# Stick-breaking logits: zero-padded products against two 64-row products

## The chip, the cores and the metric

One core of one Trainium2 chip runs the whole program. The metric is the device time of one execution in microseconds. An engine is named by the profile's short names: PE multiplies matrices (PEld is its weight load), DVE is VectorE, ACT is ScalarE, POOL is GpSimd, SP issues most of the DMAs.

## The reference

Two transformer blocks run one after the other over 512 tokens of width 1024, all in float32. The first block's mixer has two halves of 8 heads of 64: RWKV-7 (a recurrence over time) and stick-breaking attention. Then come an output projection and 32 experts, two for each token. The second block has HGRN-2 and forgetting attention as its mixer, and 16 experts. The change touches stick-breaking attention, and only its first product:

```python
z = jnp.einsum('bhqd,bhkd->bhqk', qb, kb) * scale        # d = 64, blocks of 128 queries
log_rest = jnp.where(strict, jax.nn.log_sigmoid(-z), 0.0)
suffix = lax.cumsum(log_rest, axis=3, reverse=True) - log_rest
weights = jnp.where(strict, jnp.exp(jax.nn.log_sigmoid(z) + suffix), 0.0)
outs.append(jnp.einsum('bhqk,bhkd->bhqd', weights, vb))
```

Block b reads the keys up to its own end, so 128, 256, 384 or 512 of them.

## The kernel before, in words

The program is written as one long list of instructions, and a planner orders it. It keeps a queue for each engine, takes what is ready first by its place in the program, and so moves instructions far ahead of the place where they are written, as long as their data and their buffers allow it. `in_order` (L214) holds the instructions traced inside it to their written order on each engine; other instructions may still be put between them.

`mixer1` (L443) begins with the norm and the transposed input `xh`, `xl`. A projection (`proj`, L310) is 24 matmuls of 512 columns with weights `w` that SP loads in 0.5 MB pieces into three buffers; ACT and DVE split each piece into `whi` and `wlo`. `mixer1_rw_in` (L533) makes the RWKV inputs from 14 projections. Its first step after two projections reads `lw`, 0.5 MB of LoRA weights (loaded at L538, used by the matmuls of L561 and L564, whose results go through sigmoids on ACT). Then follow steps in the order `R00 R01 P0 R10 R11 A0 P1 R20 R21 A1 P2 R30 R31 A2 P3 A3`. An R step is a unit of RWKV (`rw_unit`, many small matmuls, some of them on 64 rows). P steps (`sb_proj`, L645) make queries, keys and values of head pair j: three projections. A steps (`sb_attn`, L660) are the attention of a head pair.

In `sb_proj` the queries of a pair go into `qz`, 128 rows by 2 heads by 512: head 0 stands in rows 0 to 63 of the first half, head 1 in rows 64 to 127 of the second, and two memsets on POOL (L648, L649) zero the rest. `kT` holds the keys of both heads in its 128 rows. So a product of 128 rows (L672) gives the logits of one head, the other head's rows being multiplied by zeros. It starts the accumulation in a PSUM bank; a product of the identity with the mask `causx` (L673) ends it. A float32 product is two passes on PE. From the bank DVE takes the smaller of logit and 80 into `sbz` (L675). There are two banks for all this, `sb`, taken in turn by the scores, the transposed weights, the outputs and the head norm. `qz`, `kT` and `vS` have two buffers each, so pair j shares those of pair j - 2.

At P2 the kernel also clears `yd` (L500 to L504), a buffer in DRAM of 5 MB into which the first block's experts are added much later. The source of this DMA is one of the zeroed halves of `qz`: rows 64 to 127 of the first head of pair 2, repeated along `yd`.

Of the kernel before, what the change touches and what calls it, by code (L numbers as in the profile page):

```python
# [8 lines left out]
F32 = mybir.dt.float32  # L9
# [3 lines left out]
AF = mybir.ActivationFunctionType  # L13
# [3 lines left out]
T = 512  # L17
# [17 lines left out]
def drain(gen):  # L35

    while True:
        try:
            next(gen)
        except StopIteration as e:  # L40
            return e.value
# [141 lines left out]
class Kern:  # L183
# [259 lines left out]
    def mixer1(self, after):  # L443
        nc, tc = self.nc, self.tc
        cO, cL, cA, cB = ExitStack(), ExitStack(), ExitStack(), ExitStack()
        o = self.pool("m1o", 1, cL).tile([128, KD, T], F32, name="o", tag="o")
        cP = ExitStack()
        xp = self.pool("m1x", 1, cP, "right")
        pp = self.pool("m1p", 1, cP, "right")
        xh = xp.tile([128, KD, T], R32, name="xh")  # L450
        xl = xp.tile([128, KD, T], R32, name="xl")
        sp = self.pool("m1s", 1, cL)
        ap = self.pool("m1a", 1, cA)
        AR = ap.tile([128, 4, NT, 2, 128], F32, name="AR")
        bt = ap.tile([128, 4, T], F32, name="bt")
        kt = ap.tile([128, 4, T], F32, name="kt")
        vch = ap.tile([128, 4, T], F32, name="vch")
        xg = ap.tile([128, T], F32, name="xg")
        TTc = ap.tile([128, C, 8, NT], F32, name="TTc")
        PC = ap.tile([128, 4, 16], F32, name="PC")  # L460
        lora = self.ap["lora"].rearrange("p (a b) -> p a b", a=3)
        xv = self.ap["x"].rearrange("(n p) d -> p n d", p=128)
        self.psum(mm=2, ua=2, ch=1, pq=1, sb=2)
        self.ps_names(pj=("mm", "mm", "sb", "sb"), at=("ua", "ua", "ch", "pq"), tr=("ua", "ua", "ch", "pq"))
        self.proj_plan(self.ap["win"], range(26))
        with ExitStack() as cN:
            p = self.norm_in(self.pool("m1n", 1, cN), pp, xv, xh, xl)
        self.consts(sp, "m1")
        self.causx = self.cbf(sp, "causx")
        bp = self.pool("m1b", 1, cB)  # L470
        self.mixer1_rw_in(bp, bp, pp, p, xh, xl, AR, bt, kt, vch, xg, TTc, PC, lora)
        cB.close()
        up = self.pool("m1u", 1, cA)
        g2 = up.tile([128, 512], F32, name="g2")
        nc.sync.dma_start(g2, lora[:, 2])
        self.ps_names(pj=("mm", ))
        S = [[up.tile([128, 2, 64], F32, name=f"S{g}{i}") for i in range(2)] for g in range(2)]
        for g in range(2):
            nc.vector.memset(S[g][0], 0.0)
        qkv, before = {}, iter(())  # L480

        def shift_pools():
            cP.close()
            self.h = self.pool("hres", 1, None, "right").tile([128, NT, D], F32, name="h")
            self.crow = ExitStack()
            nrow = self.pool("rows", 1, self.crow, "right")
            self.st = nrow.tile([128, 4, NT], F32, name="st")
            self.ring_open(1)
            self.mo.ring[3] = nrow
            wo = self.wo_load(self.ap["wout"])  # L490
            for n in range(NT):
                nc.sync.dma_start(self.h[:, n], xv[:, n])
            return wo


        for step in "R00 R01 P0 R10 R11 A0 P1 R20 R21 A1 P2 R30 R31 A2 P3 A3".split():
            kind, j = step[0], int(step[1])
            if kind == "P":
                qkv[j] = self.sb_proj(pp, sp, j, xh, xl)
                if j == 2:  # L500
                    self.yd = tc.dram_tile([ZROW[1], D], F32, name="yd1")
                    zeros = qkv[j][0][64:128, 0]
                    nc.sync.dma_start(self.yd.rearrange("(p a) (d c) -> p (a d) c", p=64, c=T),
                                      zeros[:, None, :].to_broadcast([64, ZROW[1] // 32, T]))  # L504
                if j == 3:
                    wo = shift_pools()
            elif kind == "A":
                self.sb_attn(sp, j, qkv.pop(j), o, ("sb",))
            else:
                g = int(step[2])  # L510
                unit = self.rw_unit(up, j, g, S[g], o, AR, bt, kt, vch, xg, g2, TTc, PC)
                next(unit)
                drain(before)
                next(unit)
                before = unit
                if (j, g) == (3, 1):
                    drain(unit)
                    cA.close()
        st = self.out_start(o, wo, (0, 1, 2, 4, 5, 6, 7), (3,), (("mm", "mm"), ("ua", "ua"), ("ch", "pq")), cO)
        self.dbg("o", o)  # L520
        cL.close()
        after(st)
        self.out_finish(st, "mm", "sb", ("ch", "ua", "ua", "pq"))
        cO.close()
# [119 lines left out]

    def sb_proj(self, pp, tp, j, xh, xl):  # L645
        nc = self.nc
        qz = tp.tile([128, 2, T], F32, name="qz", bufs=2)
        nc.gpsimd.memset(qz[64:128, 0], 0.0)  # L648
        nc.gpsimd.memset(qz[0:64, 1], 0.0)  # L649
        p = self.proj(pp, 14 + 3 * j, xh, xl)  # L650
        for hh in range(2):
            s = slice(64 * hh, 64 * hh + 64)
            nc.scalar.activation(qz[s, hh], p[s], AF.Copy, scale=0.125)
        kT = tp.tile([128, T], F32, name="kT", bufs=2)
        nc.scalar.activation(kT, self.proj(pp, 15 + 3 * j, xh, xl), AF.Copy)
        vS = tp.tile([128, NT, 128], F32, name="vS", bufs=2)
        self.to_tok(tp, self.proj(pp, 16 + 3 * j, xh, xl), vS, "sb")
        return qz, kT, vS

    def sb_attn(self, tp, j, qkv, o, tags):  # L660


        nc = self.nc
        qz, kT, vS = qkv
        ot = tp.tile([128, T], F32, name="hno", bufs=1)

        def scores(b):
            N = 128 * (b + 1)
            w = []
            for hh in range(2):  # L670
                p = self.rot(tags)
                nc.tensor.matmul(p[:, :N], qz[:, hh, b * 128:(b + 1) * 128], kT[:, :N], start=True, stop=False)  # L672
                nc.tensor.matmul(p[:, N - 128:N], self.identb, self.causx, start=False, stop=True)  # L673
                z = tp.tile([128, T], F32, name="sbz", bufs=2)
                nc.vector.tensor_scalar(z[:, :N], p[:, :N], 80.0, None, op0=OP.min)  # L675
                e = tp.tile([128, T], F32, name="sbe", bufs=2)
                nc.scalar.activation(e[:, :N], z[:, :N], AF.Exp)
                nc.scalar.activation(e[:, :N], e[:, :N], AF.Ln, bias=self.eps[:, 2:3])
                S = tp.tile([128, T], F32, name="sbS", bufs=4)
                nc.vector.tensor_tensor_scan(out=S[:, :N][:, ::-1], data0=self.eps[:, 2:3].to_broadcast([128, N]),  # L680
                                             data1=e[:, :N][:, ::-1], initial=0.0, op0=OP.mult, op1=OP.add)
                nc.vector.tensor_tensor(S[:, :N], z[:, :N], S[:, :N], OP.subtract)
                nc.scalar.activation(S[:, :N], S[:, :N], AF.Exp)
                w.append(S)
            return w

        self.blocks(scores, lambda b, w: self.weighted(tp, tags, b, w, vS, ot))
        self.head_norm(tp, tags, ot, o[:, j], self.c("sbg", j, j + 1))

    def blocks(self, scores, weighted):  # L690

        w = scores(NT - 1)
        for b in reversed(range(NT)):
            nx = scores(b - 1) if b else None
            weighted(b, w)
            w = nx
# [1354 lines left out]
```

## Time and profile before

| | |
|---|---|
| median of 3 runs | 1418.19 us (1415.84 to 1419.23) |
| the profiled execution | 1419.25 us, span 1417.5 us |
| PE busy | 1291.9 us (91% of the span) |
| DVE, ACT, POOL busy | 838.1, 701.4, 409.8 us |
| mean granted clock of PE | 0.964 |

A matmul is shown longer than the time by which it holds back the next one; the distance of the starts is what counts. "x2" in a row of the timeline means two instructions in one stretch. The granted clock is a share of 2.4 GHz.

### The profile page before, as it was taken

To read this page: it belongs to the slowest core of one execution; us is meant where nothing else is said; L and a number is where in the kernel's file an instruction comes from. 1 tells how busy PE (TensorE), PEld (TensorE's weight loads), DVE (VectorE), ACT (ScalarE), POOL (GpSimd) and SP (SyncE) were. 2 spreads that over 40 slices of the span, in tenths; PEclk is the share of its full clock that TensorE was granted. 3 is DMA by queue.
4 is the path that set the end of the run, shared out by engine and by line. 5 is a ranking of instruction groups with operands and counts; after the bars stand their busy time and mean duration, and the time that the engine had idled before them with its cause. 6 is when DMAs were issued, how large, how long until landed. Compare 5 with 4: busy or idle time off the path is not lost.

```text
span 1417.5 us, 20480 instructions
## 1 busy us (share of the span) xinstructions
PE 1291.9 (91%) x7792; PEld 930.9 (66%) x7792; DVE 838.1 (59%) x1432; ACT 701.4 (49%) x1217; POOL 409.8 (29%) x329
## 2 busy tenths in 40 slices
PE   7999999999998899999469899999997999999993
PEld 5776766766697555554257677777795666666662
DVE  4578867556556222000065756566736898898895
ACT  6533433243644122221164555555545788888883
POOL 1000134242103101110357102010124455555455
PEclk9999999999999899999879999999997999999997
DMA  5222350000485999999922121212286999889943
GB/s 189 75 83 81 94 123 2 1 1 1 162 324 194 360 418 420 417 419 420 259 87 76 45 75 34 87 31 88 78 363 224 315 365 382 316 337 390 385 150 143
DMA packets 54452, 283.93 MB, mean 200 GB/s; under 512 B 8849, under 2 KB 9745, under 8 KB 28738
## 3 DMA queue, kind: packets, MB, share of 16 engines
q1 hardware_dynamic: 43634, 254.75, 48.0%
q0 software_dynamic: 9840, 26.39, 5.9%
q8 instruction: 66, 1.08, 0.3%
q10 hardware_dynamic: 864, 1.31, 0.3%
q14 instruction: 48, 0.39, 0.1%
HBM read 270.70 MB, written 22.29 MB: 207 GB/s over the span
## 4 chain that ended last, share of the span: by engine, by line
PE 69%; DVE 12%; DMA 11%; ACT 3%; issue 2%; POOL 1%; SPq 0%; DVEq 0%; POOLq 0%; ACTq 0%
PE mm L322 13%; PE ua L1911 4%; PE ua L1909 4%; PE ua L1910 4%; PE mm L1719 4%; DMA ew<-in_e1down_dram 3%; DMA ew<-in_e1up_dram 3%; PE ua L1663 2%; PE sb L322 2%; PE sb L1852 2%; PE sb L1851 2%; PE sb L1853 2%; PE sb L715 2%; DMA ew<-in_e1gate_dram 2%; DVE elo L1633 1%
## 5 line engine op out<-in xcount | busy, mean ns | idle before, releaser
L1633 DVE TENSOR_TENSOR elo<-ew,ehi 128x1024 fp32r<-128x1024 f32 x147 | 229.6, 1603 | 31.7 <-ACT ehi L1632 20.5
L1632 ACT ACTIVATE ehi<-ew 128x1024 fp32r<-128x1024 f32 x192 | 202.5, 1058 | 59.7 <-PE ua L1910 41.0
L322 PE MATMUL mm<-xh,whi 128*128 128x512 f32 (+1 forms) x384 | 156.7, 408 | 4.0 <-DVE hq L1147 3.7
L322 PE MATMUL mm<-xl,whi 128*128 128x512 f32 (+1 forms) x384 | 154.4, 402 | 0.5 <-DVE xl L354 0.3
L322 PE MATMUL mm<-xh,wlo 128*128 128x512 f32 (+1 forms) x384 | 153.2, 399 | 0.0
L1633 POOL TENSOR_TENSOR elo<-ew,ehi 128x1024 fp32r<-128x1024 f32 x45 | 124.5, 2767 | 63.0 <-ACT ehi L1632 60.9
L1719 PE MATMUL mm<-ew,xTh 128*64 128x256 f32 x1024 | 118.9, 386 | 6.3 <-DMA ew<-in_e1up_dram 4.6
L1911 PE MATMUL ua<-elo,xTh 128*96 128x512 f32 x256 | 103.1, 403 | 8.4 <-DVE elo L1633 8.4
L1719 PEld LDWEIGHTS mm<-ew,xTh 128*64 128x64 f32 x1024 | 73.5, 139 | 47.2 <-DMA ew<-in_e1up_dram 5.9
L1723 DVE TENSOR_TENSOR hh<-hh,mm 128x256 f32<-128x256 f32 x16 | 6.7, 421 | 163.1 <-ACT hh L1722 163.1
L1909 PE MATMUL ua<-ehi,xTh 128*96 128x512 f32 x256 | 102.3, 400 | 0.6 <-ACT xTh L1621 0.6
L1910 PE MATMUL ua<-ehi,xTl 128*96 128x512 f32 x256 | 102.1, 399 | 0.0
L296 ACT ACTIVATE whi<-w 128x1024 fp32r<-128x1024 f32 x53 | 55.9, 1056 | 92.5 <-PE mm L322 73.8
L297 DVE TENSOR_TENSOR wlo<-w,whi 128x1024 fp32r<-128x1024 f32 x52 | 63.8, 1228 | 51.7 <-ACT whi L296 51.5
L1604 POOL DMA_INDIRECT xg<-xd,idx x32 | 36.4, 1138 | 196.5 <-PE sb L1617 118.7
L322 PEld LDWEIGHTS mm<-xh,whi 128*128 128x128 f32 x384 | 74.0, 193 | 23.4 <-DVE hq L1147 5.4
L322 PEld LDWEIGHTS mm<-xl,whi 128*128 128x128 f32 x384 | 74.1, 193 | 16.8 <-issue 3.5
L322 PEld LDWEIGHTS mm<-xh,wlo 128*128 128x128 f32 x384 | 74.1, 193 | 16.1 <-issue 2.2
L1663 PE MATMUL ua<-ew,hT 128*64 128x512 f32 x240 | 66.4, 600 | 1.2 <-ACT hT L1774 1.1
L1911 PEld LDWEIGHTS ua<-elo,xTh 128*96 128x96 f32 x256 | 42.0, 164 | 30.2 <-DVE elo L1633 11.2
L1722 ACT ACTIVATE hh<-mm 128x256 f32<-128x256 f32 x16 | 6.1, 383 | 112.4 <-PE mm L1719 112.4
L1171 POOL TENSOR_TENSOR hAT<-hAT,hmt 128x512 f32<-128x512 f32 x16 | 22.1, 1381 | 119.0 <-DVE hmt L1170 118.4
(640 smaller groups left out, 3034.2 us busy)
## 6 DMA issues: line engine op xcount, KB each, us to landing
ew<-in_e1up_dram SPq DMA_DIRECT2D x32, 1024.0 KB
ew<-in_e2up_dram SPq DMA_DIRECT2D x32, 1024.0 KB
ew<-in_e2gate_dram SPq DMA_DIRECT2D x32, 1024.0 KB
ew<-in_e2down_dram SPq DMA_DIRECT2D x32, 1024.0 KB
ew<-in_e1gate_dram SPq DMA_DIRECT2D x31, 1024.0 KB
ew<-in_e1down_dram SPq DMA_DIRECT2D x30, 1024.0 KB
w<-in_win_dram SPq DMA_DIRECT2D x53, 512.0 KB
ew<-in_wout_dram SPq DMA_DIRECT2D x8, 1024.0 KB
```

Of the source, the lines that this page charges most:

```text
L296: nc.scalar.activation(hi, s, AF.Copy)
L297: (eng or nc.vector).tensor_tensor(lo, s, hi, OP.subtract)
L322: mm = lambda w, x, start=False, stop=False: nc.tensor.matmul(p[:, s], w[:, k], x[:, k, s], start=start, stop=stop, skip_group_check=parts ...
L715: nc.tensor.matmul(po[d, 0:128], v[:, kb, d], wT[hh][:, kb * 128:(kb + 1) * 128], start=kb == 0, stop=kb == b)
L1604: return self.nc.gpsimd.indirect_dma_start(out=xg, out_offset=None, in_=mo.xd, in_offset=bass.IndirectOffsetOnAxis(ap=idx[:, u:u + 1], axi ...
L1632: self.hi = nc.scalar.activation(hi, s, AF.Copy)
L1633: self.lo = (nc.gpsimd if pool else nc.vector).tensor_tensor(lo, s, hi, OP.subtract)
L1663: nc.tensor.matmul(p[hs(a)], hT[:, k, hs(a)], w[a][:, k * 1024 + d * 512:k * 1024 + d * 512 + 512], start=k == 0, stop=k == 1)
L1719: nc.tensor.matmul(d[hs(a)], xT[:, k, hs(a)], w[2 * m + a][:, k * 256:k * 256 + 256], start=k == 0, stop=k == KD - 1)
L1909: nc.tensor.matmul(p, xh[:, kk], hi[:, s], start=kk == 0, stop=False)
L1910: nc.tensor.matmul(p, xl[:, kk], hi[:, s], start=False, stop=False)
L1911: nc.tensor.matmul(p, xh[:, kk], lo[:, s], start=False, stop=kk == KD - 1)
```

## The change

The queries of both heads go into one tile `qT` of 128 rows, unpadded. A new function `products` gives both heads' logits of a block: it takes two banks, starts both with the mask, and then adds for each head a product over its own 64 rows, all held in order. The memsets go, and two copies on ACT become one. The fill of `yd` gets a source of its own, `zrow`, 64 rows of zeros, written by a memset where the fill is issued. The forgetting attention of the second block keeps its padded form.

```diff
                 if j == 2:
                     self.yd = tc.dram_tile([ZROW[1], D], F32, name="yd1")
-                    zeros = qkv[j][0][64:128, 0]
+                    zeros = sp.tile([64, T], F32, name="zrow", bufs=1)
+                    nc.gpsimd.memset(zeros, 0.0)
                     nc.sync.dma_start(self.yd.rearrange("(p a) (d c) -> p (a d) c", p=64, c=T),
                                       zeros[:, None, :].to_broadcast([64, ZROW[1] // 32, T]))
...
     def sb_proj(self, pp, tp, j, xh, xl):
         nc = self.nc
-        qz = tp.tile([128, 2, T], F32, name="qz", bufs=2)
-        nc.gpsimd.memset(qz[64:128, 0], 0.0)
-        nc.gpsimd.memset(qz[0:64, 1], 0.0)
-        p = self.proj(pp, 14 + 3 * j, xh, xl)
-        for hh in range(2):
-            s = slice(64 * hh, 64 * hh + 64)
-            nc.scalar.activation(qz[s, hh], p[s], AF.Copy, scale=0.125)
+        qT = tp.tile([128, T], F32, name="qT", bufs=2)
+        nc.scalar.activation(qT, self.proj(pp, 14 + 3 * j, xh, xl), AF.Copy, scale=0.125)
...
         def scores(b):
             N = 128 * (b + 1)
             w = []
-            for hh in range(2):
-                p = self.rot(tags)
-                nc.tensor.matmul(p[:, :N], qz[:, hh, b * 128:(b + 1) * 128], kT[:, :N], start=True, stop=False)
-                nc.tensor.matmul(p[:, N - 128:N], self.identb, self.causx, start=False, stop=True)
+            for p in self.products(qT, kT, b, self.causx, tags):
                 z = tp.tile([128, T], F32, name="sbz", bufs=2)
...
+    def products(self, q, k, b, mask, tags):
+
+        nc = self.nc
+        N = 128 * (b + 1)
+        banks = [self.rot(tags) for _ in range(2)]
+        with self.in_order():
+            for p in banks:
+                nc.tensor.matmul(p[:, N - 128:N], self.identb, mask, start=True, stop=False, skip_group_check=True)
+            for hh, p in enumerate(banks):
+                s = slice(64 * hh, 64 * hh + 64)
+                nc.tensor.matmul(p[:, :N], q[s, b * 128:(b + 1) * 128], k[s, :N], start=False, stop=True, skip_group_check=True)
+        return banks
```

## Rows read from the trace of the kernel before

**Rows 1.** Busy time by stretch: PE, PEld, DVE, ACT, POOL, granted clock, DMA, GB/s

```profile
31.00:43.00 12.00, 12.00 (x40) 7.26 (x39) 3.68 (x4) 9.94 (x14) 0.20 (x1) 1.00 0.00 0
43.00:118.00 75.00, 74.31 (x356) 58.32 (x355) 54.39 (x88) 29.79 (x42) 7.29 (x12) 1.00 0.29 87
...
170.00:370.00 200.00, 193.57 (x1585) 135.88 (x1583) 122.85 (x269) 76.36 (x166) 63.66 (x95) 1.00 0.13 30
```

**Rows 2.** What PE waited for, 20 to 404 us: total, times, longest

```profile
PE ua L845 <- DVE uRp L805: 4.9, 6, 1.2
```

**Rows 3.** Instructions that touch the tile qz: durations, first and last start

```profile
L672 PE MATMUL sb<-kT,qz x64: 270/484/956, 135.4 to 394.8; 128*128 128x512 f32 x16, 128*128 128x384 f32 x16, 128*128 128x256 f32 x16, 128*128 128x128 f32 x16
L653 ACT ACTIVATE qz<-mm x8: 570/592/594, 123.4 to 364.8; 64x512 f32<-64x512 f32 x8
L648 POOL MEMSET qz<- x4: 519/521/523, 1.0 to 256.1; 64x512 f32 x4
```

**Rows 4.** PE in order of time from 192.6: start, duration, instruction

```profile
192.64 1.02 PE L672 MATMUL sb<-kT,qz 128*128 128x512 f32 x2
193.50 1.05 PE L792 MATMUL ua<-uY,uTT 128*128 128x128 f32 x8
194.39 0.22 PE L673 MATMUL sb<-bf_causx,bf_ident 128*128 128x128 bf16 x1
```

**Rows 5.** PE at 188: two heads on 64 rows each

```profile
188.36 0.70 PE L758 MATMUL ua<-AR,kt 64*128 64x256 f32 x4
```

**Rows 6.** PE from 169: one head on 64 rows between projections

```profile
169.25 0.39 PE L322 MATMUL mm<-xl,whi 128*128 128x512 f32 x1
169.56 0.70 PE L758 MATMUL ua<-AR,kt 64*128 64x256 f32 x2
170.19 0.50 PE L322 MATMUL mm<-xh,wlo 128*128 128x512 f32 x1
170.53 0.40 PE L322 MATMUL mm<-xh,whi 128*128 128x512 f32 x1
```

**Rows 7.** PE from 157: projections with three transposes between

```profile
157.56 0.48 PE L322 MATMUL mm<-xh,whi 128*128 128x512 f32 x1
...
158.44 0.40 PE L322 MATMUL mm<-xh,wlo 128*128 128x512 f32 x1
```

**Rows 8.** The copy out of the logits' bank: durations

```profile
L675 DVE TENSOR_SCALAR sbz<-sb x32: 280/478/691, 139.6 to 395.2; 128x512 f32<-128x512 f32 x8, 128x384 f32<-128x384 f32 x8, 128x256 f32<-128x256 f32 x8, 128x128 f32<-128x128 f32 x8
```

**Rows 9.** POOL in order of time: two of the four stretches of memsets

```profile
2.11 0.52 POOL L648 MEMSET qz<- 64x512 f32 x1
...
163.84 0.52 POOL L648 MEMSET qz<- 64x512 f32 x1 [55.26 <-PE sb L673]
```

**Rows 10.** DMAs issued by SP in order of time

```profile
5.49 9.34 SPq L287 DMA_DIRECT2D w<-in_win_dram  x2
21.75 0.33 SPq L538 DMA_DIRECT2D lw<-in_lora_dram  x1
...
164.39 0.63 SPq L503 DMA_DIRECT2D yd<-qz  x1
...
178.79 17.61 SPq L287 DMA_DIRECT2D w<-in_win_dram  x2
```

**Rows 11.** DMA rate from 160 to 200 us, one number for each microsecond

```profile
GB/s 0 0 0 0 160 311 215 211 207 201 207 205 207 201 213 207 215 201 207 205 207 207 209 205 207 199 207 207 207 199 203 252 283 264 154 16 0 160 336 29
```

**Rows 12.** The same from 0 to 40 us

```profile
GB/s 0 38 233 324 303 274 385 414 426 414 426 418 399 422 123 70 303 152 0 0 0 0 41 262 221 78 254 184 25 193 332 0 0 0 0 0 0 0 0 0
```

**Rows 13.** PE at 31: the first read of lw

```profile
31.03 1.02 PE L561 MATMUL ua<-wa,lw 128*128 128x512 f32 x2
```

**Rows 14.** ACT at 41: the split of the next projection's weights

```profile
41.16 1.05 ACT L296 ACTIVATE whi<-w 128x1024 fp32r<-128x1024 f32 x1
```

**Rows 15.** PE after an idle stretch at 137, and the clock granted then

```profile
139.40 1.42 PE L672 MATMUL sb<-kT,qz 128*128 128x512 f32 x2 [2.45 <-DVE vS L643]
...
140.20:143.40 3.20, 3.20 (x8) 1.60 (x7) 2.82 (x6) 2.69 (x4) 0.00 (x0) 0.50 0.30 122
```

More of the change, by code (lines that the diff above doesn't have):

```diff
@@ L657, in sb_proj @@
         self.to_tok(tp, self.proj(pp, 16 + 3 * j, xh, xl), vS, "sb")
-        return qz, kT, vS
+        return qT, kT, vS
     def sb_attn(self, tp, j, qkv, o, tags):
         nc = self.nc
-        qz, kT, vS = qkv
+        qT, kT, vS = qkv
         ot = tp.tile([128, T], F32, name="hno", bufs=1)
```

## The prediction

> **What bounds the kernel now.** I read the page first, then busy time by stage, then what TensorE (PE) waits for, then the stretch that the diff touches in order of time. The page gives PE 91% of the span. By stage the first mixer is PE's: it is busy 12.00 of 12 us from 31 to 43, 74.31 of 75 us up to 118, and 193.57 of 200 us from 170 to 370 [rows 1]. Its longest named wait from 20 to 404 us is 4.9 us in six pieces, for VectorE inside the RWKV units [rows 2]. So here a microsecond of PE work is worth nearly a microsecond of the end, and so is a microsecond in which PE stands still. Nothing in this stretch has slack to give: what comes later (output projection, weight prefetch, experts) starts when the mixer's buffers come free, and moves with it.
>
> **The products.** The 64 matmuls of the logits are 32 products (4 head pairs, 4 query blocks, 2 heads) of two passes each [rows 3]. A pair of passes over 512 columns takes 193.50 - 192.64 = 0.86 us, 0.43 a pass [rows 4], so 0.43, 0.32, 0.21 and 0.11 us a pass for 512 to 128 columns. One head pair now costs 4 x (0.43 + 0.32 + 0.21 + 0.11) = 4.28 us. On 64 rows each, can two run at once? The RWKV units already have that shape: four passes of 256 columns, for two heads, take 0.70 us at 188.36 [rows 5], and two passes for one head take the same 0.70 at 169.56 [rows 6]. So yes: two heads cost one. That saves 2.14 us a head pair, 8.5 us in four.
>
> It has a price. Around one 64-row visit, from the projection matmul before it to the second after it, 170.53 - 169.25 = 1.28 us pass [rows 6]. Two projection matmuls at 0.23 and two passes at 0.21 make 0.88, so the visit costs 0.40. The same with full-height work (three transposes at 0.11): 158.44 - 157.56 = 0.88 against 0.46 + 0.32, so 0.10 [rows 7]. A visit costs 0.30 us more, and there are 16 (one for each block of each head pair): 4.8 us. Net, if each pair stays together: 8.5 - 4.8 = 3.7 us saved. For 128-column blocks it is a loss (0.21 saved, 0.30 paid).
>
> The Trainium skill, "TensorEngine Tiling (Array Packing)", section Tiling Modes, speaks against the change: changing the tiling mode drains the engine; its section Overview promises up to 2x for 64 rows. By the 2x alone the sum would be -8.5 us, with the drain as the rows have it -3.7 us.
>
> Do pairs stay together? The planner is free to put other work between them: the instructions of `in_order` come in order, not side by side. At 193.50 it put eight RWKV matmuls between a product and its mask, which came at 194.39 [rows 4]. I count 10 such of the 16 products of the second and third head pair, none in the first and the last, which run with no RWKV units beside them. So perhaps 5 of 16 pairs come apart. A pair together saves 0.53 - 0.30 = 0.23 on average; a pair apart saves nothing and pays two visits, 0.60: -11 x 0.23 + 5 x 0.60 = +0.5 us. I take 0 for PE. The ends are -3.7 (all together) and, with all 8 pairs of the second and third head pair apart, -8 x 0.23 + 8 x 0.60 = +3.0.
>
> **The small edits.** Both masks now go first, so the first product waits for two free banks, not one; behind it in PE's queue stands everything else. The wait is one VectorE copy out of the second bank, 0.69 us at most [rows 8], which the planner covers with projections where it has them; taken at 0, and without cover in the last head pair's step 4 x 0.69 = 2.8 at most. Eight memsets of 0.52 us go and one comes [rows 3]; they lie on POOL, which stands idle 55 us before one of them [rows 9]: 0. Two copies of 64 rows on ScalarE, 0.59 us each [rows 3], become one of 128 (estimate: as long, for as many columns), 0.6 us less four times, beside a PE that is busy: 0, at most -2.4 if each delayed PE.
>
> **The zero fill.** This is where I expect the time. A write of zeros (1280 rows of 1024 floats, 5.24 MB) clears the buffer in DRAM where the experts will add up. Before, its source is a zeroed part of `qz` of the third head pair. That buffer is the one of the first, so its memset waits 55 us for the first pair's last product and runs at 163.84 [rows 9]. The DMA leaves at 164.39 [rows 10], as soon as the memset is done, though the program writes it after the third pair's projections and the whole of the second pair's attention. So nothing holds it but its source. The new source, `zrow`, is a buffer of its own: nothing holds its memset. The memsets of the second head pair's `qz`, written as late in the program, ran at 2.11 [rows 9]. So the fill will be ready at 1 to 3 us, and leaves when SP has nothing earlier to issue: behind the weight load of 5.49, while the next one (the second of that row) waits for a buffer until 14.5, and before `lw` (the LoRA weights) at 21.75 [rows 10].
>
> What stands behind it? Issued from SP, the loads go through one queue. At 160 to 200 the fill runs at about 206 GB/s, so 25.5 us; the weight load issued at 178.79 [rows 10] adds nothing to the rate until 191 [rows 11]: it waits for the fill to end. At the start the first loads keep the DMA full until about 14.4 us [rows 12]. So the fill runs from 14.4 to 40. Then come a weight load of 0.52 MB (1.25 us at 420 GB/s, the rate of the first loads) and `lw` (as much): `lw` is there at 42.5 to 43. Before, PE read it at 31.03 [rows 13]. The stall is 12 us.
>
> Can PE do something else? One projection's weights are ready: its 5.5 us could be moved ahead. But afterwards it is missing: the next weights' split on ScalarE comes after the sigmoids that need `lw`, and ran at 41.16, 10.1 us after the first read of `lw` [rows 13, 14]; the projection of 37.5 to 43 covers that gap now. From 42.8 it would end at 54 instead of 42.2: 11.8 us late all the same. So 11.5 to 12 either way; I take 12. The bounds are 0 (the fill still leaves after `lw`) and 14 (all 28 us from the fill's issue at 164.39 to its end at 192 count, from the first loads' end at 14.4 on).
>
> A PE that stands still also loses clock: after 2.45 us without work the granted clock was 0.50 (1.2 GHz) from 140.20 to 143.40 [rows 15]. Once more after the stall: 3.2 us at half speed, +1.6 us (0 to 3.2).
>
> What the fill frees later, 166 to 192, nobody waits for: 0.
>
> **The sum.** The profiled run took 1419.25 us (span 1417.5, 1.75 around it): + 12 + 1.6 + 0 = 1432.9. It lies 1.1 above the median of the three runs, 1418.19, so I forecast 1431.8, say 1431.
>
> **The rivals.**
> - *The heads pay and the fill does no harm* (the other side). The fill's place decides: issued after `lw`, that is later than 21.75, it stands before nothing that is needed soon, as now at 164. Then -3.7 at best: 1414.5. For it: the rate of two heads is measured. Against it: nothing in the program holds the fill, and half the pairs of the middle steps come apart. 0.08.
> - *The fill does no harm and the visits eat the gain*: by the row of 0.30 a visit and pairs that come apart, 0 to +3: 1418 to 1421. 0.10. If the heads did not run at once in this place after all (the change not doing what it says), nothing is saved and the visits are paid, + 4.8: 1423.
> - *The fill is early but costs half*: `lw` gets ahead of it, or the engines serve both, or PE finds more to do; PE stalls some 5 us: 1424. For it: the queue is read from one place of the trace only. 0.10.
>
> **How the numbers follow.** Forecast 0.72, the others 0.08, 0.10, 0.10. The forecast's own range is 1426 to 1436: stall 10 to 14, clock 0 to 3.2, PE -3.7 to +3. Reaching down over the case that costs half and part of the third, the range is 1420 to 1436. A difference below 0.3% (4.3 us) can't be told from none here. Slower: 0.72, 0.08 of the case that costs half and 0.01 of the third, 0.81; within: the rest of these two, 0.11; faster: 0.08.
>
> **What would show it.** In the changed kernel's SP view the fill stands before `lw`, at 6 to 10 us; the DMA rate reads 206 GB/s from about 14 to 40; PE waits for `lw` or has a gap of some 11 us between 31 and 45, then 0.50 clock; everything behind is 11 to 14 us later. The products: the four passes of two heads start in pairs, within a few ns. Wrong if the fill stands at 100 us or later, or if `lw` lands near 25 us though the fill left first.

## The result, and the profile after

The changed kernel takes 1439.16 us (median) against 1418.71 for the kernel before in the same comparison: 1.0144 times as long, interval [1.0123, 1.0165]. Forecast were 1431, in a range up to 1436: slower, as said, but by 20.5 us, not by 13. One of the four runs of the changed kernel took 3025.74 us; the median of the other three is 1438.02, 19.3 us more than before. The profiled execution took 1438.02 us (span 1436.2), the one before 1419.25: 18.8 more, and these 18.8 us are what the traces have to explain.

The loss is where it was expected, ahead of the attention. Busy time by stretch, with the columns of [rows 1]:

```profile
31.00:43.00 12.00, 5.48 (x25) 4.20 (x23) 0.75 (x1) 1.32 (x2) 0.00 (x0) 0.90 0.96 220
43.00:118.00 75.00, 67.19 (x276) 49.04 (x276) 44.46 (x69) 32.15 (x45) 5.99 (x11) 0.90 0.28 85
170.00:370.00 200.00, 191.60 (x1578) 133.76 (x1578) 127.25 (x287) 70.63 (x155) 62.12 (x96) 1.00 0.04 13
```

PE, full before, is busy 5.48 of the 12 us up to 43, and the DMA engines, which stood idle, are busy 0.96 of the time. What PE waits for (total, times, longest), beside [rows 2], has two lines that were not there:

```profile
PE ua L562 <- DMA w<-in_win_dram: 9.7, 1, 9.7
PE sb L322 <- ACT whi L296: 4.2, 1, 4.2
```

The first is put down to a weight load; what these matmuls read is `lw`. Neither line stands among the waits of the kernel before. In order of time, SP's queue beside [rows 10], and under it PE beside [rows 13]:

```profile
5.44 9.43 SPq L287 DMA_DIRECT2D w<-in_win_dram  x2
14.91 0.63 SPq L504 DMA_DIRECT2D yd<-zrow  x1
21.61 6.37 SPq L539 DMA_DIRECT2D lw<-in_lora_dram  x1
28.08 5.03 SPq L287 DMA_DIRECT2D w<-in_win_dram  x2
```

```profile
46.17 2.05 PE L562 MATMUL ua<-wa,lw 128*128 128x512 f32 x2 [9.69 <-DMA w<-in_win_dram]
...
54.58 1.02 PE L565 MATMUL pq<-wa,lw 128*128 128x512 f32 x2
59.78 0.80 PE L322 MATMUL sb<-xh,whi 128*128 128x512 f32 x1 [4.19 <-ACT whi L296]
```

The fill leaves at 14.91 instead of 164.39, ahead of `lw`. From 10 to 50 us the DMA rate reads, beside [rows 11, 12]:

```profile
GB/s 422 422 403 421 180 70 152 342 379 319 223 209 203 201 201 215 203 201 201 215 203 201 209 209 217 201 201 213 205 201 201 238 348 389 410 299 57 25 0 0
...
yd<-zrow SPq DMA_DIRECT2D x1, 5120.0 KB, 27.6
```

Its plateau near 205 GB/s runs from 21 to 41, and the fill is done 27.6 us after its issue, at 42.5. `lw` follows: of the 16 landing signals that the trace has for it, 15 come at 43.22 to 44.53 and the last at 45.83. PE reads it at 46.17 instead of 31.03. Two stretches of the clock (the columns again those of [rows 1]):

```profile
43.00:46.00 3.00, 0.00 (x0) 0.00 (x0) 0.00 (x0) 0.00 (x0) 0.00 (x0) 0.50 0.92 366
46.00:49.00 3.00, 2.83 (x4) 1.31 (x5) 0.00 (x0) 0.69 (x1) 0.00 (x0) 0.50 0.07 27
52.00:55.00 3.00, 3.00 (x8) 1.33 (x7) 0.00 (x0) 2.31 (x5) 0.00 (x0) 1.00 0.00 0
...
58.00:61.00 3.00, 1.22 (x2) 0.50 (x2) 2.19 (x2) 3.00 (x5) 0.20 (x1) 0.50 0.00 0
61.00:64.00 3.00, 2.79 (x8) 2.21 (x8) 2.35 (x4) 0.87 (x2) 0.00 (x0) 0.50 0.59 164
```

PE starts the LoRA products at 0.50 (1.2 GHz), after 9.69 us without work. It is at 1.00 again from 50.8 on, waits 4.19 us for a weight split, and is at 0.50 once more.

The products themselves are what the diff says, beside [rows 3]:

```profile
L693 PE MATMUL sb<-kT,qT x64: 272/481/693, 158.4 to 414.3; 64*128 64x512 f32 x16, 64*128 64x384 f32 x16, 64*128 64x256 f32 x16, 64*128 64x128 f32 x16
L649 ACT ACTIVATE qT<-mm x4: 577/580/584, 142.2 to 381.5; 128x512 f32<-128x512 f32 x4
```

Where the two kernels stand apart, from the start of the same instruction in both timelines (later in the changed kernel, us):

| what | before | later by |
|---|---|---|
| first read of `lw` (PE) | 31.03 | 15.1 |
| the projection that waits at 59.78 (PE) | 43.36 | 16.4 |
| the projection behind it (PE) | 49.9 | 18.8 |
| the sixth weight split (ACT) | 50.0 | 18.7 |
| the 19th weight split (ACT) | 133.3 | 18.8 |
| the 26th weight split (ACT) | 362.7 | 16.9 |
| first sum of the output projection (DVE) | 425.4 | 19.3 |
| end of the span | 1417.5 | 18.8 |

By 50 us of the kernel before, all is lost. Some 2 us come back while the attention runs and are gone at its end.

### The profile page after: what moved, and what is told of

Its sections match the earlier page's. It is cut to its first block, busy times and chain, and to the rows that moved or that the text cites. A ratio compares the mean times of both kernels' runs of the same rounds, so it can differ in the third digit from the quotient of the medians.

```text
span 1436.2 us, 20470 instructions
## 1 busy us (share of the span) xinstructions
PE 1291.3 (90%) x7792; PEld 929.5 (65%) x7792; DVE 839.0 (58%) x1432; ACT 698.5 (49%) x1213; POOL 403.0 (28%) x322
## 4 chain that ended last, share of the span: by engine, by line
PE 71%; DVE 14%; DMA 7%; ACT 3%; issue 3%; POOL 1%; SPq 0%; DVEq 0%; ACTq 0%; POOLq 0%
PE mm L322 11%; PE mm L1725 6%; PE ua L1917 4%; PE ua L1915 4%; PE ua L1916 4%; PE ua L1669 4%; PE sb L1858 2%; PE sb L1857 2%; PE sb L1859 2%; PE sb L721 2%; PE sb L322 2%; DMA ew<-in_e1up_dram 2%; DMA ew<-in_e1down_dram 2%; PE mm L884 1%; DVE elo L1639 1%
## 5 line engine op out<-in xcount | busy, mean ns | idle before, releaser
L787 POOL TENSOR_TENSOR uVbd<-uV,pc_m 128x256 f32<-128x256 f32 x32 | 23.2, 750 | 115.2 <-ACT uV L777 115.2
```

## The experiments

The theory: the early fill makes the whole loss, because it stands ahead of `lw` in SP's one queue; the products give and take about the same. The rival: the 64-row visits and the masks that wait for two banks cost the time. Ratios are to the kernel before on the same chip.

**The fill put back (late_fill).**

```diff
...
-                    zeros = sp.tile([64, T], F32, name="zrow", bufs=1)
+                    zeros = sp.tile([128, T], F32, name="qT", bufs=3)[0:64]
...
```

(and `qT` with three buffers). 

> The changed kernel with one thing undone: the zeros of the fill lie again in a buffer that the first head pair's logits have to leave (a third buffer of qT), so the fill waits as in the kernel before; the side-by-side products stay. Theory (the fill's place makes the whole loss; the products give and take about the same): the fill leaves near 164 us, lw is read at 31, no stretch of 0.50 clock between 43 and 63, and the time is 1419 (1416 to 1422), no more than 0.2% from the kernel before. Rival (the products, with their 64-row visits and masks that wait for two banks, make the loss, and the stall in the fill would be made up later): 1434 to 1439, as the changed kernel.

Measured: 1417.78 us, 0.9987 [0.9976, 0.9998]. PE in order of time reads `lw` where it did before:

```profile
30.96 1.03 PE L562 MATMUL ua<-wa,lw 128*128 128x512 f32 x2
```

The tile `yd` in the same kernel (durations in ns, first and last start):

```profile
L504 SPq DMA_DIRECT2D yd<-qT x1: 627/627/627, 221.5 to 221.5; - x1
```

The fill left later than I said, 221.5 and not 164; nobody waits for it there either. The whole loss is gone with the fill's place, and the rival of the products falls.

**The early fill alone (fill_only).**

```diff
+                if j == 1:
+                    zeros = qkv[j][0][64:128, 0]
                 if j == 2:
                     self.yd = tc.dram_tile([ZROW[1], D], F32, name="yd1")
-                    zeros = qkv[j][0][64:128, 0]
```

> The kernel before with one thing added: the fill takes its zeros from the second head pair's buffer, whose memset ran at 2.11 us, so nothing holds it; the products stay zero-padded on 128 rows. Theory (the fill's place): the fill leaves before lw, lw is read at about 46 instead of 31, PE loses 15 us and some 3.5 us to 0.50 clock, 1437.5 (1434 to 1441). Rival (the products): 1417 to 1422.

Measured: 1437.87 us, 1.0135 [1.0120, 1.0150], with the same two waits on PE in order of time:

```profile
46.06 2.05 PE L562 MATMUL ua<-wa,lw 128*128 128x512 f32 x2 [10.66 <-DMA w<-in_win_dram]
...
60.35 0.80 PE L322 MATMUL sb<-xh,whi 128*128 128x512 f32 x1 [4.18 <-ACT whi L296]
```

One part done alone brings the loss, the same part undone takes it away.

**Half of it early (half_fill).** The fill is split in two DMAs of 2.62 MB; one takes its zeros from `zrow`, the other from the third buffer of `qT`.

```diff
...
+                    nc.sync.dma_start(yv[:, :half], early[:, None, :].to_broadcast([64, half, T]))
+                    nc.sync.dma_start(yv[:, half:], zeros[:, None, :].to_broadcast([64, half, T]))
...
```

(In the expectations the projection that PE has ready during the wait is called the second, the next one the third; the third starts at 43.36 in the kernel before, not at 43.1.) 

> The changed kernel, but only half of the fill (2.62 MB) takes its zeros from the free buffer and leaves early; the other half waits for the first head pair as in the kernel before. PE's order is that of the changed kernel, with the second projection ahead of the LoRA products. Theory (queue order): the half takes 12 us instead of 23.9, lw lands near 32 instead of 44, so PE goes on without a gap after that projection, at 36.3; what is left is that ScalarE splits the next weights only after the sigmoids, 10.1 us after the first read of lw, so the third projection starts 2 us after that, at 48.4 instead of 43.1 in the kernel before: 5.3 us late, with 0 to 2 us of 0.50 clock: 1424 to 1427. Rival A (the loss goes with the bytes): half of 20.5, 1429. Rival B (an early fill of any size costs the same, because its place in SP's queue or PE's changed order does it): 1436 to 1439.

Measured: 1424.73 us, 1.0042 [1.0028, 1.0057]. PE in order of time:

```profile
36.50 1.03 PE L566 MATMUL ua<-wa,lw 128*128 128x512 f32 x2
...
47.72 0.80 PE L322 MATMUL sb<-xh,whi 128*128 128x512 f32 x1 [4.19 <-ACT whi L296]
```

Half the bytes cost some 6 us, not 10: the wait for `lw` is gone (the projection ran in its place, and PE went on at 36.50 with no gap), and the wait for the next split stays, 4.19 us as in the full case, since it hangs on the sigmoids and not on the DMA. So a stall that is covered by moving work ahead comes up again where that work is missing.

**Only the masks first (masks_first).** The kernel before, in the new order of passes, still zero-padded.

```diff
...
+            banks = [self.rot(tags) for _ in range(2)]
+            with self.in_order():
+                for p in banks:
+                    nc.tensor.matmul(p[:, N - 128:N], self.identb, self.causx, start=True, stop=False, ...)
+                for hh, p in enumerate(banks):
+                    nc.tensor.matmul(p[:, :N], qz[:, hh, b * 128:(b + 1) * 128], kT[:, :N], start=False, stop=True, ...)
...
```

> The kernel before with only the order of the logits' passes changed: both masks first, then the two heads' products one behind the other, each still zero-padded over 128 rows; the fill waits as before. It parts the two terms of the products: the price of the new order, and what two heads side by side give. Theory (the terms nearly cancel, order costs nothing): within 2 us of the kernel before, and 0 to 3 us slower than the changed kernel with the late fill. Rival (the wait for two free banks costs PE what the side-by-side heads save): 4 to 8 us slower than the kernel before.

Measured: 1416.57 us, 0.9988 [0.9979, 0.9998]. The order costs nothing, against the rival. But it is not slower than late_fill either (0.9987), as I had expected: no gain from the heads side by side is seen in the time. The two runs can be laid beside each other: PE's order around the products is the same in both. PE in order of time at the second head pair, first masks_first, then late_fill:

```profile
206.36 0.23 PE L673 MATMUL sb<-bf_causx,bf_ident 128*128 128x128 bf16 x1
206.43 1.94 PE L675 MATMUL sb<-kT,qz 128*128 128x512 f32 x4
208.29 0.70 PE L761 MATMUL ua<-AR,kt 64*128 64x256 f32 x2
208.92 0.33 PE L771 MATMUL ua<-pc_c,AR 128*128 128x128 f32 x1
```

```profile
207.56 0.23 PE L690 MATMUL sb<-bf_causx,bf_ident 128*128 128x128 bf16 x1
207.72 1.13 PE L693 MATMUL sb<-kT,qT 64*128 64x512 f32 x4
208.69 0.59 PE L764 MATMUL ua<-AR,kt 64*128 64x256 f32 x2
209.21 0.33 PE L774 MATMUL ua<-pc_c,AR 128*128 128x128 f32 x1
```

From the first pass to the next instruction, four passes of 512 columns hold PE for 1.86 us padded and for 0.97 side by side. That count leaves out what a change of height costs elsewhere (the mask stands 0.07 us ahead of the first pass padded, 0.16 side by side), so I count from the mask to an instruction of full height further on: 2.56 us against 1.65, 0.91 saved. The neighbours `ua<-AR,kt` work on 64 rows themselves here. The 384 columns of the third head pair stand between work of full height:

```profile
309.18 0.29 PE L673 MATMUL sb<-bf_causx,bf_ident 128*128 128x128 bf16 x2
309.31 1.51 PE L675 MATMUL sb<-kT,qz 128*128 128x384 f32 x4
...
311.46 0.48 PE L322 MATMUL mm<-xl,whi 128*128 128x512 f32 x1
```

```profile
310.18 0.28 PE L690 MATMUL sb<-bf_causx,bf_ident 128*128 128x128 bf16 x2
310.38 0.92 PE L693 MATMUL sb<-kT,qT 64*128 64x384 f32 x4
...
312.14 0.48 PE L322 MATMUL mm<-xl,whi 128*128 128x512 f32 x1
```

2.28 us against 1.96: 0.32 saved. Read in the same way, also between work of full height, the first pair's 256 columns save 0.09 (1.22 against 1.13, from 155.39 and 156.60), and its 128 columns lose 0.12 (1.04 against 1.16, from 163.46 and 164.59). The 384 columns of the second pair, whose heads come apart, lose 0.7.

**The fill behind lw (fill_behind_lw).**

```diff
+                    with tc.issue_after(self.lwd.ins):      # the DMA of lw
                         nc.sync.dma_start(self.yd...
...
```

> The changed kernel with the fill put directly behind lw in SP's queue, ahead of the fifth weight load; PE's order comes back to that of the kernel before. Theory (what stands behind the fill in the queue waits for its 24 us): lw is there in time and read at 31, but the fill runs from 22 to 46, the next weights land at 47 to 48, their split takes 1.05 us and more, and the third projection starts near 49.4 instead of 43.1: 6 us late, with 0 to 1.6 us of 0.50 clock: 1425 (1423 to 1428). Rival (only the LoRA products are urgent enough, so a fill behind lw harms nothing): 1417 to 1420.

Measured: 1426.47 us, 1.0051 [1.0033, 1.0069]. SP and PE in order of time:

```profile
20.77 0.33 SPq L540 DMA_DIRECT2D lw<-in_lora_dram  x1
21.15 0.63 SPq L505 DMA_DIRECT2D yd<-zrow  x1
...
56.81 0.79 PE L322 MATMUL mm<-xh,whi 128*128 128x512 f32 x1 [4.51 <-ACT whi L296]
```

`lw` is in time (read at 30.05), and what comes next in the queue is late: the size came out, the place one projection later than I said. The fill ended at 48.4 by the DMA records, and the weights behind it landed at 51.6, not at 47 to 48. ACT split them only at 55.72, 4.1 us later, after steps of the RWKV inputs that the planner had put ahead of them. How much of the 8.2 us found behind this is the transfer, and how much that order, is not separated.

**The fill in another queue (fill_pool_queue).** Same time, same source, issued by POOL.

```diff
+                    with tc.issue_after(self.plo):          # POOL's split of the first weights
+                        nc.gpsimd.dma_start(self.yd...
...
```

> The changed kernel with the fill issued by POOL on its own queue, behind POOL's split of the first weights, so at about the same time (14.5 us) as in the changed kernel; lw and the weights stay on SP's queue. Theory (the order within SP's one queue holds lw, not the DMA engines): lw lands 2 to 5 us after its issue at 21.6, PE reads it at 31, the weights behind it come in time: 1417 to 1421. Rival (the DMA engines themselves are taken by the fill, whichever queue it is in): lw lands at 40 or later, 1434 to 1439. In between (the two queues share evenly and the weights behind lw come late): 1422 to 1428.

Measured: 1417.35 us, 0.9999 [0.9984, 1.0013]. POOL and PE in order of time:

```profile
14.54 1.40 POOL L506 DMA_DIRECT2D yd<-zrow  x1
...
33.83 1.10 PE L564 MATMUL ua<-wa,lw 128*128 128x512 f32 x2 [3.40 <-DMA lw<-in_lora_dram]
```

The DMA rate from 10 to 50 us, to be laid beside that of the changed kernel:

```profile
GB/s 418 414 407 426 123 66 238 336 303 221 201 197 209 197 209 201 217 201 197 315 410 332 336 397 369 328 418 369 238 209 205 213 184 45 0 0 115 344 66 86
```

So it is the order in SP's queue: with the fill elsewhere, `lw` passes it. But not freely: `lw`, issued at 21.01, landed at 33.48, where it took 3.4 us from issue to landing in late_fill. By the packet records its first packet started only at 29.04. Until then the fill ran alone at some 205 GB/s; from 29 to 38 both queues moved data, at up to 418 GB/s together. The Trainium skill, "DMA: Bandwidth & Descriptors", section Issuing engines are not separate DMA queues, says that DMAs of all issuing engines run on the same 16 DMA engines and interleave; the trace agrees from 29.04 on. Why `lw` moved nothing in the 8 us before is not shown. At 133 us this kernel was still 2.9 us behind the one before. In the profiled executions 2.8 us came back at 782 to 791 us, after a wait of 2.9 us that both have: this one ran at 1.00 there, the kernel before at 0.50. So the equal times do not show that this place is free.

**PE kept at work (awake_pe).**

```diff
+        w = self.ps("ua")
+        with self.in_order():
+            for _ in range(10):
+                nc.tensor.matmul(w, self.ident, xg, start=True, stop=True)
         for j in range(4):
             p = self.ps("at")
```

> The changed kernel, with ten 128x512 matmuls of no use (8.6 us of PE at full clock, into a bank that nobody reads) put ahead of the LoRA products, beside the second projection, so that PE works while it waits for lw; all else in the same order. Theory (part of the loss is clock): lw still comes at 46, but the LoRA products take 6.5 us at 1.00 instead of 9.3 at 0.50, so the third projection starts near 57 instead of 59.8: 1435 to 1436; a second stretch of 0.50 after the next wait may go too, 1433.5 at best. Rival (the clock is no part of it, the products would wait for something else): 1438 to 1440.

Measured: 1434.72 us, 1.0110 [1.0088, 1.0133]; the four runs lie as far apart as 1431.91 and 1438.34, so the reading is from the trace. PE in order of time:

```profile
45.58 1.10 PE L566 MATMUL ua<-wa,lw 128*128 128x512 f32 x2 [0.91 <-DMA w<-in_win_dram]
...
51.67 1.02 PE L569 MATMUL pq<-wa,lw 128*128 128x512 f32 x2
56.87 0.79 PE L322 MATMUL sb<-xh,whi 128*128 128x512 f32 x1 [4.18 <-ACT whi L296]
```

From the first read of `lw` to the next projection: 56.87 - 45.58 = 11.3 us, in the changed kernel 59.78 - 46.17 = 13.6. The first half-speed stretch cost 2.3 us. The second, after the wait of 4.18, came here too, so the best case of the expectation did not.

**The wait of the masks (late_v_bank).** late_fill, with the transposes of v in bank `ch` for the first and the last pair.

```diff
-        self.to_tok(tp, self.proj(pp, 16 + 3 * j, xh, xl), vS, "sb")
+        self.to_tok(tp, self.proj(pp, 16 + 3 * j, xh, xl), vS, "sb" if j in (1, 2) else "ch")
```

> The kernel with the late fill, and the transposes of v of the first and the last head pair in a bank of their own (ch) instead of one of the two sb banks for which both masks have to wait. In late_fill PE stands idle 2.42 us before the first pair's second mask and 0.73 us before the last pair's, each until VectorE has copied v out, and both stretches are followed by 0.50 clock. Theory (the wait of the masks for two banks costs PE the idle and the clock after it): 2.4 + 0.7 us of idle and up to 1.7 + 1.7 us of clock go, 1413 (1411 to 1415). Rival (PE finds the next wait instead, the ScalarE and VectorE steps of the logits): 1416 to 1419.

Measured: 1419.72 us, 1.0005 [0.9994, 1.0016]. The wait for `vS` (3.1 us in late_fill) is gone, and among the waits of PE this line stands in its place:

```profile
PE sb L690 <- DVE sbz L668: 3.4, 2, 2.8
```

In late_fill it reads 1.5 us. The rival comes nearest, though it said 1416 to 1419: another wait of the chain takes over. The edit moved more than one wait: the planner put the first pair's logits at 132.3 instead of 139.5 and its copy of v at 205.5 instead of 138.6, so the run compares two orders. No version measured beats the kernel before by more than 0.13%.

**Two more executions (late_fill_2, masks_first_2).** No edit; they ask whether the clock stretches in the attention explain why executions of one kernel differ by some us. 

> The kernel with the late fill once more, for one more profiled execution. Its times ran from 1413.59 to 1420.07 us, and the one profiled, 1419.01, shows 0.50 clock after two waits, near 140 and 382 us; the kernel with only the masks first was profiled at about 1416 and shows neither. Theory (the few us between executions of one kernel are these stretches, which come in some executions and not in others): if this one takes 1413 to 1415, both stretches are missing; if 1417, one; if 1419 to 1420, both are there. Rival (the clock follows from the 64-row products, so late_fill always has both, and the spread comes from elsewhere): both are there whatever the time.

 

> The kernel before with only the masks first once more, for one more profiled execution (times so far 1414.14 to 1419.38). Theory: as for late_fill_2, the stretches of 0.50 clock near 140 and 382 us go with the time: none at 1414 to 1416, one or both at 1417 to 1420. Rival (products over all 128 rows keep the clock up): neither is there whatever the time.

late_fill_2 took 1415.83 us and has both stretches; masks_first_2 took 1414.08 and has one, at 139, where masks_first had none. So the clock neither follows the products nor, at these two places, the time: the theory fell as I had put it. What makes late_fill 3.2 us longer than late_fill_2 is mainly one stretch elsewhere. The two timelines agree within 0.4 us up to 782 us but for 1.3 in the experts; there PE waits 2.90 us in both, and then busy time and clock differ (columns of [rows 1]; first late_fill, then late_fill_2):

```profile
782.00:786.00 4.00, 3.65 (x9) 2.88 (x10) 3.97 (x8) 2.21 (x4) 0.00 (x0) 0.50 0.09 36
```

```profile
782.00:786.00 4.00, 4.00 (x18) 3.31 (x19) 3.97 (x8) 2.00 (x4) 0.00 (x0) 1.00 0.15 24
```

Over this place late_fill falls back by 2.9 us. From 791 us on late_fill_2 is 2.5 to 3.6 us ahead, 3.2 at the end.

## Why the prediction was wrong

The direction and the mechanism were right: the fill is issued early, stands ahead of `lw`, and PE waits. Two terms of the sum, the stall and the clock, were too small, each outside its own bounds, and together they left the range.

- **The fill is hoisted, ahead of lw.** Right, and shown from both sides. It left at 14.91, not at 6 to 10: the weight load that I saw waiting for a buffer until 14.5 [rows 10] went first after all, because it is older in SP's queue.
- **The stall, 12 us (bounds 0 to 14).** This is the step that failed first: 15.1, outside its own bounds. I began the transfer at 14.4, the end of the first loads; by the DMA records one more load ended at 18.3 and the fill at 42.2 (23.9 us, 1.6 less than I took). Then came `lw`, with no weight load between. I gave both together 2.5 us; `lw` alone took 3.6 from the end of the fill to its last landing signal at 45.83, 1.3 us after the fifteenth. PE began 0.3 us after that. So 2.2 of the missing 3.1 us lie in the end of the fill and the rest behind it. The upper bound had the end of the fill right (42.4) and failed on `lw` alone. Why the last part landed so late is not shown.
- **Moving a projection ahead gains nothing.** Nearly right: the planner moved it, PE worked on it to 36.3, and with the clock taken out (awake_pe) the next projection was 13.5 us late (56.87 against 43.36) for a read that was 14.55 late: 1.0 gained. I had compared the ends of the splits; in the kernel before, PE got to the projection only 1.15 us after its split was done.
- **The clock, 1.6 us (0 to 3.2).** Also too small: 2.3 us in the LoRA products (awake_pe) and 2.4 in the projection behind them (16.4 to 18.8 in the table), 4.7 together. I had counted one stretch and taken its length from [rows 15]. The second follows from my own step on the moved projection: I had seen that a gap opens where it is missing, and had not asked what the clock does after it.
- **The sum.** 15.1 + 2.3 + 2.4 - 1.0 = 18.8, as measured. The range was also narrower than its terms: their upper bounds, 14 + 3.2 + 3, lead to 1438.4 and not to 1436.
- **The products, 0 (-3.7 to +3.0).** Right: late_fill stands at 0.9987 of the kernel before, by the start of the output projection it is 0.3 us ahead of it, and masks_first, which has no side-by-side product, stands at 0.9988. The price of a visit was right as well. Between work of full height two heads side by side save 0.32, 0.09 and -0.12 us where the passes alone would save 0.64, 0.42 and 0.21 (384, 256 and 128 columns): 0.32 to 0.33 a visit, forecast 0.30. What I had not seen is that the price can vanish beside other work on 64 rows, as for the 512 columns of the second pair (0.91 saved, the passes alone 0.86). 13 of the 16 pairs stay together, not 11. In the stretch from 170 to 370, where the clock is 1.00 in both, PE is busy 192.44 us in late_fill and 192.59 in masks_first (193.57 before), so there the heads side by side give next to nothing. The Trainium skill, "TensorEngine Tiling (Array Packing)", section Tiling Modes, has the drain that comes with a change of mode; the rows agree that there is a price, these 0.32 to 0.33 us a visit.
- **The wait for two banks, 0.** Right: masks_first is not slower.
- **What the fill frees at 166 to 192, 0.** Right: at 164 or 221 nobody waits for it.

## What to carry to other kernels

When a transfer loses the thing that held it, ask first where the planner will put it, then count everything behind it in that queue, each load in its turn and until its last part has landed. An idle gap can cost PE more than its length: two gaps here were followed by work at 1.2 GHz that took 2.3 and 2.4 us longer. A gap closed by work from later opens again where that work is missing, with its own stretch. The price of a short piece of other work is read between two instructions well ahead of it and well behind it, in two runs that have the same order there; a count from its first pass leaves a part of the price out.

## What the runs showed of the hardware

A load of 0.5 MB issued while a 5.24 MB fill ran in another queue took 12.5 us to land (fill_pool_queue), against 3.4 alone (late_fill); in 8.0 of them it moved no packet, though the fill moved only some 205 GB/s and the two together later reached 418. Right behind the fill in one queue, 15 of its 16 landing signals came by 44.53 us and the last at 45.83 (after); alone, all 16 came within 0.4 us (late_fill). A visit of two heads on 64 rows between work of full height costs 0.32 to 0.33 us (late_fill against masks_first). After the same wait of 2.90 us the granted clock fell to 0.50 in one execution and stayed at 1.00 in another of the same kernel (late_fill, late_fill_2); this one place made 2.9 of the 3.2 us between them.
